# A gated-DeltaNet layer on one core: one dense v tile, 64-row state products in shared PSUM banks, plain matrices for the triangular solve

## Chip, cores and metric

The kernel runs on one core of a Trainium2 chip. The metric is the device time of one execution in microseconds; 3 runs of the kernel before have a median of 1622.08 us (1618.85 to 1623.61). A core has five engines with a queue each: TensorE (PE, its weight loads are listed as PEld), VectorE (DVE), ScalarE (ACT), GpSimd (POOL) and SyncE (SP, which issues the DMAs). They run side by side and meet at semaphores.

## The reference, cut to what matters

Two layers over 256 latent and 256 context tokens of 1024 channels: a state-space layer, then a gated DeltaNet layer, each followed by an MLP. The change lies in the DeltaNet layer, which runs in two directions over 16 value heads in chunks of 64 tokens:

```python
lower = jnp.where(strict, jnp.einsum('nbhcd,nbhsd->nbhcs', k_beta, k_b) * decay, 0.0)
t_mat = lax.linalg.triangular_solve(lower + eye, eye, left_side=True, lower=True, unit_diagonal=True)
u = jnp.einsum('nbhcs,nbhse->nbhce', t_mat, v_b * beta_b[..., None])
w = jnp.einsum('nbhcs,nbhsd->nbhcd', t_mat, k_beta * jnp.exp(g_b)[..., None])
...
def advance(state, w_i, u_i, kend_i, glast_i):
    v_new = u_i - jnp.einsum('bhcd,bhde->bhce', w_i, state)
    new_state = state * jnp.exp(glast_i)[..., None, None] + jnp.einsum('bhcd,bhce->bhde', kend_i, v_new)
    return v_new, new_state
```

For each head and direction there are 8 chunks in a row (4 of context, 4 of latents), so 8 steps that depend on each other.

## The kernel before

Two 64-token chunks, one of each direction, share the 128 partitions: a step n of a head works on chunk n of the forward direction and on its mirror chunk of the backward one, and a chunk sits in rows 0 to 63 or 64 to 127 by its parity. The layer is made of tasks, Python generators that issue instructions piece by piece:

- `gdn_proj` (line 1610): projections from the hidden stream, three fp32r products each (high and low halves of the weights), with `w_load` and `w_split` that load the weights and split them into `whi` (ScalarE) and `wlo` (GpSimd).
- `post_qk`, `post_v`, `post_z` and `prep_kk`: convolution, normalisation and transposes behind the projections.
- `gdn_t` (line 1752): the inverse of the triangular matrix for a pair of heads and one direction, by five doubling steps and two corrections. X is the decay exponent, N the matrix, `nb` its fp16 copy and `lo` the rest. In each doubling step `T` is a transpose of `U` (DVE), `ap` a product with `nb` (TensorE), `A` the masked result (DVE), `up` a product with `A`, and `U` its copy (ACT). `bd` multiplies with a block-diagonal 128 by 128 `nb` in 8 products of 64 columns; `quad` in 16 products of 64 by 64, a row half and a column half each. There are 16 `gdn_t`: 8 pairs, 2 directions.
- `gdn_chain` (line 1837): the recurrence of one head. In a step, `ks` is the product of the key with the state S (`c<-S,kt` in the trace), `r0` the remainder (DVE), `vp` the product of the inverse with r0 (`c<-r,ub`, or `c<-vs,ub` in a head's first step), `v2` its scaled copy (ACT), `kv` the product of the key with v2 (`c<-v,kn`), and the new S two DVE operations on kv. Latent steps add `qs`, `op` and `vn` for the output. Every row of v belongs to one direction; v2 is a 128 by 2 by 128 tile with a column block for each direction, in which the other direction's rows stay zero (`gdn_zero`, line 2041, zeroes these tiles and those of nb and lo once).
- `gdn_out`: the output projection (`wo`), the last work of the layer.

Three chains run at a time (`NCH` is 3), each in a PSUM bank of its own: `self.cp` (line 1491) gives chain x the column blocks ks, kv0 and kv1 of bank `c{x}`. The third bank also serves early projections.

Which task issues next is decided by `drive` (line 323): a model of engine times (`Clock`) finds for each task when its next piece could start, and the earliest one goes, ties by priority (chains 0, solves 1, projections 4, output projection 5). So a change of instructions changes the order of the whole layer on every engine. Each engine then runs its queue in that order. Line 273 is the helper that records every operation, so the trace's rows all carry it and are told apart by tile names.

Of the kernel before, what the change touches and what calls it, by code (L numbers as in the profile page):

```python
# [8 lines left out]
F32 = mybir.dt.float32  # L9
F32R = mybir.dt.float32r  # L10
F16 = mybir.dt.float16
BF16 = mybir.dt.bfloat16
AF = mybir.ActivationFunctionType
OP = mybir.AluOpType
# [1404 lines left out]
M_INC, M_U, M_A, M_ID, M_OFF, M_G, NCONST2 = 0, 128, 256, 896, 960, 1024, 1026  # L1419

NPR, NT, NQK, NCH, NHI, NRB, LZ = 1, 2, 4, 3, 2, 3, 2
# [36 lines left out]
class K3(K2):  # L1458
# [3 lines left out]
    def gdn_init(self, pool):  # L1462

        nc, V, G = self.nc, self.nc.vector, self.nc.gpsimd
        P = self.g = pool
# [7 lines left out]
        for n in range(2):  # L1473
            t = P.tile([128, 524], F32, name=f"pp{n}")
# [11 lines left out]
        for n in range(2):  # L1486
            for L, name in ((self.nb, "nb"), (self.lo, "lo")):
                L.append(P.tile([128, 8, 128], F16, name=f"{name}{n}"))
        self.cb = [self.bank(f"c{n}", f"c{n}", bufs=1) for n in range(3)]

        self.cp = [(b[:, 0:128], b[:, 128:256], b[:, 256:384]) for b in self.cb] + [tuple(b[:, 384:512] for b in self.cb)]
# [6 lines left out]
        for x in range(NCH):  # L1498
            self.v2.append([P.tile([128, 2, 128], F32, name=f"v2{x}{n}") for n in range(2)])
# [252 lines left out]
    def gdn_t(self, p, d, st):  # L1752

        nc, V, G = self.nc, self.nc.vector, self.nc.gpsimd
        W, B, c2 = self.gw, self.gb, self.c2
        tb = lambda name: self.bank(name, f"t{d}", bufs=1)
        B8 = lambda x: x.rearrange("p (c i) -> p c i", i=64)
        B42 = lambda x: x.rearrange("p (m h i) -> p m h i", m=4, h=2)
        mask = lambda n: c2[:, n:n + 64].unsqueeze(1).to_broadcast([128, 8, 64])
        halves = [slice(0, 64), slice(64, 128)]  # L1760

        X = B.tile([128, 512], F32, name="X")
# [5 lines left out]
        G.tensor_tensor(B8(X), B8(X), mask(M_INC + 64 * d), op=OP.add)  # L1768
# [5 lines left out]
        G.tensor_tensor(B8(N), B8(N), mask(M_ID), op=OP.add)  # L1774
# [5 lines left out]
        for h in halves:  # L1780
            nc.scalar.copy(nb[h, :, h], B8(N)[h])
        yield
        for h in halves:
            G.tensor_tensor(lo[h, :, h], B8(N)[h], nb[h, :, h], op=OP.subtract)
        G.tensor_tensor(ibd, B42(X)[:, 2:4], st["kqs"].unsqueeze(2).to_broadcast([128, 2, 2, 64]), op=OP.mult)

        def bd(out, l, r, first, last):
            for b in range(8):
                cs = slice(64 * b, 64 * b + 64)
                nc.tensor.matmul(out[:, cs], l[:, b], r[:, cs], start=first and b == 0, stop=last and b == 7, skip_group_check=True)  # L1790

        def quad(out, l, r):
            for b in range(8):
                cs = slice(64 * b, 64 * b + 64)
                for h in halves:
                    nc.tensor.matmul(out[h, cs], l[h, cs], r[h, cs] if r is not self.id16 else r[h], start=b == 0, stop=b == 7, skip_group_check=True)

        for n in range(5):
            T = B.tile([128, 512], F16, name="T", tag=f"T{d}", bufs=1)
            V.transpose(T, U)  # L1800
            yield
            ap = tb("ap")
            bd(ap, nb, T, True, True)
            A = B.tile([128, 512], F16, name="A", tag=f"A{d}", bufs=1)
            V.tensor_tensor(B8(A), B8(ap), mask(M_A + 64 * (5 * d + n)), op=OP.mult)
            yield
            up = tb("up")
            quad(up, A, U)
            U = B.tile([128, 512], F16, name="U", tag=f"U{d}")
            nc.scalar.copy(U, up)  # L1810
            yield
# [7 lines left out]
        bd(ep, nb, T0, True, False)  # L1819
        bd(ep, lo, T0, False, False)  # L1820
# [16 lines left out]
    def gdn_chain(self, p, h2, st):  # L1837
# [5 lines left out]
        ks, *kv = self.cp[x]  # L1843
# [6 lines left out]
        for n in range(8):  # L1850
# [17 lines left out]
            if n < 7:  # L1868
                v2 = self.v2[x][n % 2]
                for d in range(2):  # L1870
                    nc.scalar.activation(v2[rows[d], d], vp[rows[d]], AF.Identity, scale=self.vsc[rows[d], n, hd:hd + 1])
# [12 lines left out]
            if n < 7:  # L1884
                if x < 3:
                    kvw = self.cb[x][:, 128:384]
                    mm(kvw, kn[:, ms], v2.rearrange("p d e -> p (d e)"))
                else:
                    for d in range(2):
                        mm(kv[d], kn[:, ms], v2[:, d])  # L1890
                Sn = new("S", [128, 2, 128], 2)
                if S is None:
                    if x < 3:
                        nc.scalar.copy(Sn.rearrange("p d e -> p (d e)"), kvw)
                    else:
                        for d in range(2):
                            nc.scalar.copy(Sn[:, d], kv[d])
                else:
                    for d in range(2):
                        V.scalar_tensor_tensor(Sn[:, d], S[:, d], self.egl[:, n, d, hd:hd + 1], kv[d],  # L1900
                                               op0=OP.mult, op1=OP.add)
                S = Sn
                yield
# [137 lines left out]
    def gdn_zero(self):  # L2041

        for t in self.nb + self.lo + [t for v in self.v2 for t in v]:
            self.pin(self.nc.gpsimd.memset(t, 0.0))
            yield

    def gdn_phase(self, tmp, gb, hp, new):
# [56 lines left out]
        zero = T(self.gdn_zero(), 3, [j], "gpsimd")  # L2104
        tasks += [g, zero]
        gates(0)
        for p in range(8):
# [11 lines left out]
            tt.append([T(self.gdn_t(p, d, st[p]), 1, [g, zero, kk] + ago(tt, 1)[d:d + 1] + ago(ch, NRB), "gpsimd") for d in range(2)])  # L2119
# [142 lines left out]
```

## Time and profile before

| | |
|---|---|
| median of 3 runs | 1622.08 us |
| the profiled execution, its own time | 1624.46 us |
| its span, first to last instruction | 1622.7 us |
| granted TensorE clock over the span | 0.947 |
| TensorE busy | 1469.8 us (91%) |
| DVE, ACT, POOL busy | 1096.8, 776.3, 650.6 us |
| recurrence layer | from about 760 to 1421 us |

Times in rows are microseconds from the span's start, unless marked ns. Busy time is the union of an engine's instructions; matmuls are pipelined, so a row's duration is longer than the time until the next one begins, and the difference of two starts tells how long a group holds the engine. An fp32 product is two instructions (two passes) on the chip.

### The profile page before, as it was taken

To read this page: it belongs to the slowest core of one execution; us is meant where nothing else is said; L and a number is where in the kernel's file an instruction comes from. 1 tells how busy PE (TensorE), PEld (TensorE's weight loads), DVE (VectorE), ACT (ScalarE), POOL (GpSimd) and SP (SyncE) were. 2 spreads that over 40 slices of the span, in tenths; PEclk is the share of its full clock that TensorE was granted. 3 is DMA by queue.
4 is the path that set the end of the run, shared out by engine and by line. 5 is a ranking of instruction groups with operands and counts; after the bars stand their busy time and mean duration, and the time that the engine had idled before them with its cause. 6 is when DMAs were issued, how large, how long until landed. Compare 5 with 4: busy or idle time off the path is not lost. (4 is left out here: it accounts for less than half of the span.)

```text
span 1622.7 us, 31318 instructions
## 1 busy us (share of the span) xinstructions
PE 1469.8 (91%) x12370; PEld 1115.6 (69%) x12370; DVE 1096.8 (68%) x2036; ACT 776.3 (48%) x1635; POOL 650.6 (40%) x590
## 2 busy tenths in 40 slices
PE   6898558999999999997978898989998999989998
PEld 2355436777777788886767676767776665689997
DVE  6978858774334344447999967686978875667766
ACT  3243456553223232325556655656675755554543
POOL 3962003642333233334776734353544400024432
PEclk7999779998999999998979999989998999999999
DMA  9887743554455533322222211111111102536552
GB/s 274 290 270 250 110 91 132 173 192 146 139 173 178 177 118 104 104 78 81 93 66 66 66 53 60 40 60 44 56 63 57 41 25 96 196 121 198 181 193 91
DMA packets 76771, 200.77 MB, mean 124 GB/s; under 512 B 8784, under 2 KB 29008, under 8 KB 76368
## 3 DMA queue, kind: packets, MB, share of 16 engines
q1 hardware_dynamic: 76112, 197.78, 38.5%
q8 instruction: 97, 1.59, 0.4%
q10 hardware_dynamic: 512, 0.98, 0.3%
q14 instruction: 50, 0.41, 0.1%
HBM read 192.71 MB, written 6.03 MB: 122 GB/s over the span
## 5 line engine op out<-in xcount | busy, mean ns | idle before, releaser
L273 ACT CAST whi<-wraw 128x1024 fp32r<-128x1024 f32 x221 | 225.3, 1045 | 239.5 <-PE w L273 149.2
L273 POOL TENSOR_TENSOR wlo<-wraw,whi 128x256 fp32r<-128x256 f32 (+1 forms) x221 | 208.3, 970 | 289.5 <-ACT whi L273 271.9
L273 DVE TENSOR_TENSOR wlo<-wraw,whi 128x1024 fp32r<-128x1024 f32 (+1 forms) x189 | 225.1, 1220 | 61.7 <-ACT whi L273 60.3
L273 PE MATMUL w<-hh,whi 128*128 128x256 f32 (+1 forms) x512 | 169.9, 335 | 0.0
L273 PE MATMUL w<-hl,whi 128*128 128x256 f32 (+1 forms) x512 | 168.9, 331 | 0.0
L273 PE MATMUL w<-hh,wlo 128*128 128x256 f32 (+1 forms) x512 | 168.4, 331 | 0.4 <-DVE wlo L273 0.4
L273 PE MATMUL w<-whi,h1l 128*128 128x512 f32 x384 | 148.4, 390 | 0.0
L273 PE MATMUL w<-wlo,h1h 128*128 128x512 f32 x384 | 148.4, 389 | 0.0
L273 POOL TENSOR_TENSOR sq<-rl 128x512 f32<-128x512 f32 (+1 forms) x64 | 62.4, 975 | 213.7 <-ACT rl L273 213.7
L273 PE MATMUL w<-whi,h1h 128*128 128x512 f32 x384 | 147.7, 393 | 0.0
L273 PE MATMUL proj<-hh,whi 128*128 128x256 f32 (+1 forms) x360 | 132.4, 368 | 7.4 <-ACT pp L273 6.7
L273 DVE TENSOR_TENSOR ma<-w,g 128x512 f32<-128x512 f32 x96 | 65.3, 687 | 105.3 <-PE w L273 105.2
L273 PE MATMUL proj<-hh,wlo 128*128 128x256 f32 (+1 forms) x360 | 127.5, 354 | 1.3 <-POOL wlo L273 1.3
L273 PE MATMUL proj<-hl,whi 128*128 128x256 f32 (+1 forms) x360 | 127.5, 354 | 0.0
L273 DVE SCALAR_TENSOR_TENSOR cacc<-pp,cw,cacc 128x520 f32<-128x520 f32 (+1 forms) x128 | 112.4, 879 | 9.6 <-ACT cacc L273 8.1
L273 POOL TENSOR_TENSOR xr<-xr,ma 128x512 f32<-128x512 f32 x56 | 79.5, 1421 | 89.2 <-DVE ma L273 89.2
L273 DVE TENSOR_TENSOR h1l<-sq,h1h 128x512 fp32r<-128x512 f32 (+1 forms) x64 | 35.5, 555 | 114.4 <-POOL sq L273 111.9
L273 ACT ACTIVATE v<-c,vsc 64x128 f32<-64x128 f32 x224 | 80.7, 362 | 62.4 <-PE c L273 57.6
L273 PEld LDWEIGHTS w<-hh,whi 128*128 128x128 f32 x512 | 98.0, 192 | 14.9 <-DVE wlo L273 2.5
L273 PEld LDWEIGHTS w<-hl,whi 128*128 128x128 f32 x512 | 98.2, 192 | 10.7 <-issue 1.9
L273 PEld LDWEIGHTS w<-hh,wlo 128*128 128x128 f32 x512 | 97.9, 192 | 10.2 <-issue 0.8
L273 ACT ACTIVATE rl<-w 128x512 f32<-128x512 f32 (+1 forms) x64 | 31.3, 489 | 130.1 <-PE w L273 120.8
(316 smaller groups left out, 3480.2 us busy)
## 6 DMA issues: line engine op xcount, KB each, us to landing
wraw<-in_w_dram SPq DMA_DIRECT2D x128, 512.0 KB, 4.3
adaw<-in_ada_w_dram SPq DMA_DIRECT2D x92, 512.0 KB, 4.8
wraw<-in_w_in_dram SPq DMA_DIRECT2D x48, 512.0 KB, 3.2
wraw<-in_w_glu_dram SPq DMA_DIRECT2D x32, 512.0 KB, 3.3
wraw<-in_w_out_dram SPq DMA_DIRECT2D x16, 512.0 KB, 3.5
Kt<-kd SPq DMA_DIRECT2D x32, 128.0 KB, 6.2
X<-grd SPq DMA_DIRECT2D x32, 128.0 KB, 3.2
V<-in_ada_w_dram SPq DMA_DIRECT2D x4, 512.0 KB, 6.1
```

Of the source, the lines that this page charges most:

```text
L273: r = f(*args, **kw)
```

## The change

1. `v2` becomes a dense 128 by 128 tile, filled by one activation. The state product is made for each direction apart, from the 64 rows of its chunk, into 128 columns.
2. The banks are dealt out anew: `c2` holds ks and vp of all three chains (128 columns each), `c0` the states of chunks of even parity and `c1` those of odd parity, again for all three chains.
3. `nb` and `lo` become plain 128 by 512 tiles, and `bd` is gone: `quad` does all products of the solve. One ScalarE copy makes nb.
4. GpSimd's additions on X and N and its `lo` are done in pieces of 256 columns.
5. `gdn_zero` and its task are gone.

```diff
-                L.append(P.tile([128, 8, 128], F16, name=f"{name}{n}"))
+                L.append(P.tile([128, 512], F16, name=f"{name}{n}"))
...
-        self.cp = [(b[:, 0:128], b[:, 128:256], b[:, 256:384]) for b in self.cb] + [tuple(b[:, 384:512] for b in self.cb)]
+        self.cp = [tuple(self.cb[n][:, 128 * x:128 * x + 128] for n in (2, 0, 1)) for x in range(NCH)]
...
-            self.v2.append([P.tile([128, 2, 128], F32, name=f"v2{x}{n}") for n in range(2)])
+            self.v2.append([P.tile([128, 128], F32, name=f"v2{x}{n}") for n in range(2)])
...
+        quarters, two = [slice(0, 256), slice(256, 512)], [slice(0, 4), slice(4, 8)]
...
-        G.tensor_tensor(B8(X), B8(X), mask(M_INC + 64 * d), op=OP.add)
+        for b in two:
+            G.tensor_tensor(B8(X)[:, b], B8(X)[:, b], mask(M_INC + 64 * d)[:, b], op=OP.add)
...
-        G.tensor_tensor(B8(N), B8(N), mask(M_ID), op=OP.add)
+        for b in two:
+            G.tensor_tensor(B8(N)[:, b], B8(N)[:, b], mask(M_ID)[:, b], op=OP.add)
...
-        for h in halves:
-            nc.scalar.copy(nb[h, :, h], B8(N)[h])
+        nc.scalar.copy(nb, N)
         yield
-        for h in halves:
-            G.tensor_tensor(lo[h, :, h], B8(N)[h], nb[h, :, h], op=OP.subtract)
+        for c in quarters:
+            G.tensor_tensor(lo[:, c], N[:, c], nb[:, c], op=OP.subtract)
...
-        def bd(out, l, r, first, last):
-            for b in range(8):
-                cs = slice(64 * b, 64 * b + 64)
-                nc.tensor.matmul(out[:, cs], l[:, b], r[:, cs], start=first and b == 0, stop=last and b == 7, skip_group_check=True)
...
-            bd(ap, nb, T, True, True)
+            quad(ap, nb, T)
...
-        bd(ep, nb, T0, True, False)
-        bd(ep, lo, T0, False, False)
+        quad(ep, nb, T0, True, False)
+        quad(ep, lo, T0, False, False)
...
-                for d in range(2):
-                    nc.scalar.activation(v2[rows[d], d], vp[rows[d]], AF.Identity, scale=self.vsc[rows[d], n, hd:hd + 1])
+                nc.scalar.activation(v2, vp, AF.Identity, scale=col(self.vsc, n))
...
-                if x < 3:
-                    kvw = self.cb[x][:, 128:384]
-                    mm(kvw, kn[:, ms], v2.rearrange("p d e -> p (d e)"))
...
+                kv = [kvs[c % 2] for c in cs]
+                for d in range(2):
+                    mm(kv[d], kn[rows[d], ms], v2[rows[d]])
...
-        for t in self.nb + self.lo + [t for v in self.v2 for t in v]:
-            self.pin(self.nc.gpsimd.memset(t, 0.0))
-            yield
```

The order on TensorE, late in the layer, where chains stand close together. The names are those of the trace with the tile's number: c0 to c2 are the banks, S, r0, vs and v2 carry the chain's number (S2 is a state of chain 2, v201 a v2 of chain 0), and an fp32 product is one row here. Before, with three chains:

```order
L273 MATMUL c0_6466<-S0_15218,kt_12408 64x128 [waits DVE_49]
L273 MATMUL c0_6466<-S0_15218,kt_12408 64x128
L273 MATMUL c2_6468<-S2_15456,kt_13768 64x128 [waits Activation_49]
L273 MATMUL c2_6468<-S2_15456,kt_13768 64x128
L273 MATMUL c1_6467<-S1_15127,kt_12408 64x128 [waits DVE_49]
L273 MATMUL c1_6467<-S1_15127,kt_12408 64x128
L273 MATMUL qs_15181<-S1_15127,qt_12456 64x128 [waits DVE_49]
L273 MATMUL qs_15181<-S1_15127,qt_12456 64x128
L273 MATMUL op_15227<-vn0_15189,ibd0_13117 64x128 [waits DVE_49]
L273 MATMUL op_15227<-vn0_15189,ibd1_13798 64x128
L273 MATMUL c0_6466<-r00_15248,ub0_13893 64x128 [waits DVE_49]
L273 MATMUL c0_6466<-r00_15248,ub1_14627 64x128
```

In this stretch every chain writes its own bank and waits for one engine, the one that made its state or remainder.

The change, at the corresponding place, with the last two heads' chains:

```order
L273 MATMUL c2_6468<-S2_16357,kt_15009 64x128 [waits DVE_49,Activation_49]
L273 MATMUL c2_6468<-S2_16357,kt_15009 64x128 [waits DVE_49]
L273 MATMUL c1_6467<-v201_6470,kn_14878 128x128
L273 MATMUL c0_6466<-v201_6470,kn_14878 128x128
L273 MATMUL c2_6468<-r02_16380,ub0_16126 64x128 [waits DVE_49]
L273 MATMUL c2_6468<-r02_16380,ub1_16257 64x128
L273 MATMUL c2_6468<-S0_16384,kt_15009 64x128 [waits DVE_49,Activation_49]
L273 MATMUL c2_6468<-S0_16384,kt_15009 64x128 [waits DVE_49]
L273 MATMUL c0_6466<-v220_6473,kn_14878 128x128
L273 MATMUL c1_6467<-v220_6473,kn_14878 128x128
```

Both chains write ks and vp into c2. The first product with S of one chain now waits for DVE (its state) and for ACT (the other chain's v2, which ACT reads from c2). The state product is two rows into two banks.

The order on GpSimd, in the first solves. Before:

```order
L273 TENSOR_TENSOR N_7259<-N_7259,c2_6444 128x512 [waits DVE_49]
L273 TENSOR_TENSOR ibd0_7296<-X_7168,kqs_7132 128x256 [waits Activation_49]
L273 TENSOR_TENSOR ibd1_7301<-X_7171,kqs_7132 128x256
L273 TENSOR_TENSOR N_7268<-N_7268,c2_6444 128x512 [waits DVE_49]
L273 TENSOR_TENSOR lo0_6463<-N_7259,nb0_6462 64x8x64 [waits Activation_49]
L273 TENSOR_TENSOR lo0_6463<-N_7259,nb0_6462 64x8x64 [waits Activation_49,Pool_49]
L273 TENSOR_TENSOR X_8109<-X_8109,c2_6444 128x512 [waits DMAHW7_49,DMAHW6_49,Pool_49]
L273 TENSOR_TENSOR lo1_6465<-N_7268,nb1_6464 64x8x64 [waits Activation_49]
L273 TENSOR_TENSOR lo1_6465<-N_7268,nb1_6464 64x8x64 [waits Activation_49,Pool_49]
```

Here an addition on X or N is one row, and `lo` one row for each half of the partitions (in this listing c2_6444 is the table of masks, not a bank).

The change:

```order
L273 TENSOR_TENSOR N_7161<-N_7161,c2_6444 128x256 [waits DVE_49]
L273 TENSOR_TENSOR N_7161<-N_7161,c2_6444 128x256
L273 TENSOR_TENSOR N_7219<-N_7219,c2_6444 128x256 [waits DVE_49]
L273 TENSOR_TENSOR N_7219<-N_7219,c2_6444 128x256
L273 TENSOR_TENSOR X_8061<-X_8061,c2_6444 128x256 [waits DMAHW6_49,DMAHW5_49,Pool_49]
L273 TENSOR_TENSOR X_8061<-X_8061,c2_6444 128x256
L273 TENSOR_TENSOR lo0_6463<-N_7161,nb0_6462 128x256 [waits Activation_49]
L273 TENSOR_TENSOR lo0_6463<-N_7161,nb0_6462 128x256 [waits Pool_49]
```

All three are two rows of 256 columns over all partitions.

## Rows read from the trace of the kernel before

**Rows 1.** The page, busy time of TensorE (us, share of the span, instructions).

```profile
PE 1469.8 (91%) x12370; PEld 1115.6 (69%) x12370; DVE 1096.8 (68%) x2036; ACT 776.3 (48%) x1635; POOL 650.6 (40%) x590
```

**Rows 2.** Stretches: length; PE, PEld, DVE, ACT, POOL busy; clock; DMA share; GB/s.

```profile
760.00:840.00 80.00, 68.99 (x378) 58.06 (x377) 74.52 (x106) 41.17 (x91) 59.99 (x69) 0.91 0.27 87
840.00:1337.00 497.00, 455.88 (x5576) 338.21 (x5575) 390.82 (x827) 307.53 (x800) 230.29 (x242) 0.95 0.16 52
...
1350.00:1397.00 47.00, 44.87 (x273) 27.60 (x273) 26.99 (x74) 24.58 (x63) 1.71 (x2) 1.00 0.33 111
```

**Rows 3.** TensorE in order of time from 1254 us: start, duration, group.

```profile
1254.52 0.70 PE L273 MATMUL c<-v,kn 128*128 128x256 f32 x2
1255.15 0.43 PE L273 MATMUL op<-vn,ibd 64*64 64x128 f32 x4
1255.42 0.39 PE L273 MATMUL c<-r,ub 64*64 64x128 f32 x4
1255.74 0.44 PE L273 MATMUL c<-S,kt 128*64 128x128 f32 x4
1256.11 0.44 PE L273 MATMUL up<-U,A 64*64 64x64 f16 x16
1256.47 0.32 PE L273 MATMUL qs<-S,qt 128*64 128x128 f32 x1
...
1257.07 0.41 PE L273 MATMUL ap<-T,nb 128*128 128x64 f16 x8
1257.31 0.68 PE L273 MATMUL c<-v,kn 128*128 128x256 f32 x2
...
1262.31 0.41 PE L273 MATMUL ap<-T,nb 128*128 128x64 f16 x8
1262.64 0.43 PE L273 MATMUL c<-r,ub 64*64 64x128 f32 x4
```

**Rows 4.** The same view near 1094 us.

```profile
1094.22 0.59 PE L273 MATMUL c<-v,kn 128*128 128x256 f32 x2
1094.75 0.44 PE L273 MATMUL op<-vn,ibd 64*64 64x128 f32 x4
```

**Rows 5.** What TensorE waited for, 840 to 1397: us, times, longest us.

```profile
PE ap L273 <- DVE T L273: 12.8, 7, 4.5
PE c L273 <- DVE S L273: 9.5, 8, 4.8
...
PE c L273 <- DVE r L273: 3.8, 4, 2.6
PE c L273 <- ACT vn L273: 3.3, 6, 1.1
...
PE c L273 <- ACT v L273: 3.1, 7, 0.7
```

**Rows 6.** ScalarE's groups, 760 to 1400: busy us, mean ns, idle before.

```profile
L273 ACT ACTIVATE v<-c,vsc 64x128 f32<-64x128 f32 x224 | 80.7, 362 | 62.4 <-PE c L273 57.6 <-DVE cacc L273 2.0 <-DVE qss L273 0.2
...
L273 ACT CAST nb<-N 64x512 f16<-64x512 f32 x32 | 19.7, 617 | 6.5 <-POOL N L273 3.1 <-PE ep L273 2.9
```

**Rows 7.** GpSimd's groups, 760 to 1345, the same columns.

```profile
L273 POOL TENSOR_TENSOR wlo<-wraw,whi 128x256 fp32r<-128x256 f32 x184 | 152.2, 858 | 153.4 <-ACT whi L273 136.0 <-PE ap L273 9.8 <-PE kTp L273 7.2
...
L273 POOL TENSOR_TENSOR N<-N,c 128x512 f32<-128x512 f32 x16 | 23.7, 1499 | 4.0 <-DVE N L273 4.0
L273 POOL TENSOR_TENSOR X<-X,c 128x512 f32<-128x512 f32 x16 | 22.7, 1426 | 6.7 <-DMA X<-grd 5.1 <-PE kp L273 1.2
...
L273 POOL MEMSET nb<- 128x1024 f16 x2 | 1.9, 1002 | 0.0
L273 POOL MEMSET lo<- 128x1024 f16 x2 | 1.9, 950 | 0.0
L273 POOL MEMSET v<- 128x256 f32 x6 | 1.6, 308 | 0.0
```

**Rows 8.** State products from 1337 to 1421, the groups of TensorE.

```profile
L273 PE MATMUL c<-v,kn 128*128 128x256 f32 x34 | 10.9, 403 | 1.7 <-ACT vn L273 0.9 <-ACT v L273 0.6
```

More of the change, by code (lines that the diff above doesn't have):

```diff
@@ L1779, in gdn_t, with quad @@
         nb, lo = self.nb[d], self.lo[d]
-        for h in halves:
-            nc.scalar.copy(nb[h, :, h], B8(N)[h])
+        nc.scalar.copy(nb, N)
         yield
-        for h in halves:
-            G.tensor_tensor(lo[h, :, h], B8(N)[h], nb[h, :, h], op=OP.subtract)
+        for c in quarters:
+            G.tensor_tensor(lo[:, c], N[:, c], nb[:, c], op=OP.subtract)
         G.tensor_tensor(ibd, B42(X)[:, 2:4], st["kqs"].unsqueeze(2).to_broadcast([128, 2, 2, 64]), op=OP.mult)
-        def bd(out, l, r, first, last):
-            for b in range(8):
-                cs = slice(64 * b, 64 * b + 64)
-                nc.tensor.matmul(out[:, cs], l[:, b], r[:, cs], start=first and b == 0, stop=last and b == 7, skip_group_check=True)
-        def quad(out, l, r):
+        def quad(out, l, r, first=True, last=True):
             for b in range(8):
@@ L1795, in quad @@
                 for h in halves:
-                    nc.tensor.matmul(out[h, cs], l[h, cs], r[h, cs] if r is not self.id16 else r[h], start=b == 0, stop=b == 7, skip_group_check=True)
+                    nc.tensor.matmul(out[h, cs], l[h, cs], r[h, cs] if r is not self.id16 else r[h],
+                                     start=first and b == 0, stop=last and b == 7, skip_group_check=True)
         for n in range(5):
@@ L1842, in gdn_chain @@
         x = (2 * p + h2) % NCH
-        ks, *kv = self.cp[x]
+        ks, *kvs = self.cp[x]
         vp = ks
@@ L1884, in gdn_chain @@
             if n < 7:
-                if x < 3:
-                    kvw = self.cb[x][:, 128:384]
-                    mm(kvw, kn[:, ms], v2.rearrange("p d e -> p (d e)"))
-                else:
-                    for d in range(2):
-                        mm(kv[d], kn[:, ms], v2[:, d])
+                kv = [kvs[c % 2] for c in cs]
+                for d in range(2):
+                    mm(kv[d], kn[rows[d], ms], v2[rows[d]])
                 Sn = new("S", [128, 2, 128], 2)
                 if S is None:
[L1893 to L1897, printed above, removed]
+                    for d in range(2):
+                        nc.scalar.copy(Sn[:, d], kv[d])
                 else:
@@ L2039, in tail_init @@
         self.end = end
-    def gdn_zero(self):
-        for t in self.nb + self.lo + [t for v in self.v2 for t in v]:
-            self.pin(self.nc.gpsimd.memset(t, 0.0))
-            yield
     def gdn_phase(self, tmp, gb, hp, new):
@@ L2103, in gdn_phase @@
         tasks.append(T(alone(), 0, [j], "gpsimd"))
-        zero = T(self.gdn_zero(), 3, [j], "gpsimd")
-        tasks += [g, zero]
+        tasks.append(g)
         gates(0)
@@ L2118, in gdn_phase @@
                 v.append(T(self.post_v(p, h2, st[p], x), 3, [j] + ago(ch, NRB), "scalar"))
-            tt.append([T(self.gdn_t(p, d, st[p]), 1, [g, zero, kk] + ago(tt, 1)[d:d + 1] + ago(ch, NRB), "gpsimd") for d in range(2)])
+            tt.append([T(self.gdn_t(p, d, st[p]), 1, [g, kk] + ago(tt, 1)[d:d + 1] + ago(ch, NRB), "gpsimd") for d in range(2)])
             for h2 in range(2):
```

## Prediction

> **What bounds the kernel now.** I began with the page. TensorE is busy for 91% of the span [rows 1], an average over stages that says nothing of the stage that is changed. So I cut the second half into stretches by what is recorded there [rows 2]: 760 to 840 us (first projections and gates), 840 to 1337 (recurrence layer with all its helpers), and 1350 to 1397 (last chains beside output projection). In the first DVE is the full one, 74.5 of 80 us. From 840 to 1397 TensorE is: 455.9 of 497 and 44.9 of 47 us, with DVE at 79% and ACT at 62% in the former. The granted clock there is 0.95, so a tenth of the time ran at 1.2 GHz and the rest at 2.4.
>
> What does TensorE's busy time consist of? Starts of successive groups in the order of time show it [rows 3]. A group of four `c<-S` (two directions, two passes each, on two column halves of the array) holds the engine for 0.37 us until the next group begins; sixteen `up` (64 by 64, fp16) 0.36; eight `ap` (full array, fp16) 0.24 when a full-array product comes next and 0.33 when a 64 by 64 one does. The state product `c<-v,kn`, one of 112, holds it for 0.63 us, the dearest step of a chain. A quieter place has 0.53 [rows 4]. Half of that product's columns meet zeros: each v row is filled for one direction, so the full 128 by 256 product does twice the needed work.
>
> When TensorE idles, it is mostly for DVE [rows 5]: 12.8 us before `ap` for the transpose, 9.5 for S. The waits of the chains (S, r, vn, v) are 19.7 us together, at 25 places.
>
> **The change part by part.** All is against the profiled execution, 1624.46 us (span 1622.7); the median of the runs, 1622.08, lies 2.4 lower.
>
> State product: 112 products of 128 rows by 256 columns become 224 of 64 rows by 128 columns, one per direction, in two banks. No row of this trace has two products on the two row halves. The nearest are `c<-S` (two column halves, 0.37 for both directions) and `op` (64 by 64 on the diagonal, 0.27 until the next group in the same mode) [rows 3]; in both the two directions run beside each other. If row halves do the same, a group goes from between 0.53 and 0.63 down to 0.37: 112 x 0.16 = 18 us to 112 x 0.26 = 29 us less. If the second has to follow the first, it takes 0.37 + 0.27 = 0.64, which is 1 us (against 0.63) to 12 us (against 0.53) more. I take **-23 us**, the middle of the first pair, since every pair of half-size products in the rows overlaps.
>
> Solve products on plain matrices: `ap` goes from 8 full products to 16 quarter ones, 80 times. Like `up` it will hold 0.36 us, today 0.24 to 0.33: +0.03 x 80 = +2 to +0.12 x 80 = +10. `ep` has two such sets 16 times: 2 x (0.36 - 0.24) x 16 = +4 at most, and less since the second set follows in the same mode. I take **+6** for both, since most `ap` stand beside 64-row groups as in the rows, with 14 as the upper end. The Trainium skill (TensorEngine Tiling (Array Packing), section Key Properties) says that a change of tiling mode drains TensorE. The 0.24 and 0.33 of `ap` agree. By that rule alone every `ap` beside a projection pays a switch it does not pay now, which is the +14 end, and the sum below would be 8 us poorer.
>
> ScalarE: 224 activations of v on 64 rows, 362 ns each, become 112 on 128 rows; the 32 copies of N into nb (617 ns each) become 16 [rows 6]. That is 40.5 and some 10 us of ACT time, nearly all beside TensorE's work: TensorE idled 3.1 us for v and 3.3 for vn, queued behind v [rows 5]. I take **-2**, between 0 and -6.4. The first state copy of a head is split in two, 16 times, a few hundred ns, under the same cover. If ACT were late, kn's product would be the next one to wait.
>
> GpSimd: N and X are added in two pieces of 256 columns. A piece of 256 has 858 ns (`wlo`), a whole one 1499 and 1426 [rows 7]: +0.22 and +0.29 us on each solve's path, which the copy into nb gives back (-0.62, one activation in place of two). `lo`, now two pieces over 128 rows in place of two over 64, is read only by `ep`, a dozen steps later. Sum on the path -0.1 us for each of 16 solves in two lanes: **0**, with 16 x 0.5 / 2 = 4 us either way. Shorter pieces might also hold up DVE less; the rows price only whole instructions.
>
> Zeroing: ten memsets, 1.9 + 1.9 + 1.6 = 5.4 us [rows 7], vanish from GpSimd's queue while DVE sets the pace [rows 2]: **-1**, between 0 and -5.4. No DMA is added or taken away.
>
> Banks: until now every chain had a bank of its own. Now c2 holds ks and vp of all three chains, and c0 and c1 their states. A TensorE write into a bank waits for reads of it that stand earlier, whichever columns they take. In the instruction order 62 in place of 16 `c<-S` wait for ACT, 29 in place of 0 `c<-r`, 7 in place of 4 `c<-vs`, and 34 in place of 0 state products wait for DVE: 46 + 29 + 3 + 34 = 112 waits more. What is queued behind them on TensorE is everything. Price: the order of before has 112 waiting `c<-S`, 112 `c<-r` and 112 state products, and these 336 cost 19.7 us of idling [rows 5], 0.06 each; so 112 x 0.06 = **+7**. From below it is 0 (each already over), from above 112 x 0.36 (a whole read of v) = +41.
>
> Sum: -23 + 6 - 2 + 0 - 1 + 7 = -13, 1611 us for the profiled execution, **1609** against the median.
>
> **The rivals.**
> *Chain latency counts as well.* One step loses a v activation (0.36) and the longer end of the state product (0.26): 0.62 us x 7 steps x 16 heads / 3 lanes = 23 us on top, 1586. For it: TensorE's idling before state products is all for v and vn [rows 5]. Against it: from 840 on TensorE is over 90% busy, so a chain that is ready sooner finds the engine taken.
> *The freed time isn't collected.* DVE, on which TensorE waits most, gets no less work. Then only the stretch from 1337, where no projection of the layer is left and output projection soon fills the gaps, gives its part: 17 state products (34 instructions [rows 8]) x 0.26 = 4 us, 1618. Within 0.3% (about what a measurement of this kernel can tell from no change, 4.9 us).
> *Shared banks stall the engine (slower).* Place: ks of one chain behind the v read of another, as in the order shown above, where two heads strictly alternate on c2. If each new wait costs the whole 0.36 us read, 41 in place of 7: 1643. It decides from (13 + 7) / 112 = 0.18 us a wait, three times what a chain's wait costs now. Against it: a read is over in 0.36 us and other work stands between most pairs. For it: ACT has `whi` casts of a microsecond in its queue ahead of v. The Trainium skill (PSUM — Partial Sum Buffer, section on bank collisions) asks to guard PSUM by bank and quadrant and not by address; that is why disjoint columns don't help, and the order's waits agree.
> *Row halves run one after the other (slower).* The state product then gains nothing (+1 in place of -23) and `ap` stays dearer: 1633. Against it stands every overlapping pair in the rows; none is of this kind, though.
>
> **How the numbers follow.** Forecast (1609) 0.45; latency as well (1586) 0.12; not collected (1618) 0.17; stalls from banks (1643) 0.16; row halves in turn (1633) 0.10. Faster: 0.45 + 0.12 = 0.57; same 0.17; slower 0.16 + 0.10 = 0.26. The range leaves out the 0.16 of full stalls and reaches from just under the latency case to the case of row halves in turn: 1585 to 1634, which also takes in the bounds of `ap` and `ep` (+8 more), of the zeroing and of GpSimd. The faster cases by themselves span 1585 to 1617.
>
> **What would show it.** Right: a state-product group of four instructions that holds TensorE for about 0.37 us; `ap` with 16 at 0.36; v with 112 activations of some 0.36 us; TensorE's idling for chains (S, r, v, vn) within some 7 us of today's 19.7. Wrong: if the pairs of state products start 0.27 us apart, row halves don't overlap; if idling before `c<-S` and `c<-r` for ACT reaches 20 us, banks have eaten the gain; if TensorE's busy time from 840 falls by 15 us or more and the time doesn't, DVE holds the pace.

## The result, and the profile after

The changed kernel takes **1733.87 us** (median of 4 runs, 1728.69 to 1736.18) against 1622.84 for the kernel before on the same chip: a ratio of 1.0682, 95% interval 1.0649 to 1.0715, 111 us slower. The prediction, 1609 us and most likely faster, was wrong in sign, and the time lies outside its range. The profiled execution took 1733.88 us, with a span of 1732.1.

First the stretches of the changed kernel (length; PE, PEld, DVE, ACT and POOL busy; granted clock; DMA share; GB/s). The second stretch runs from 840 us to the last state of the last chain, the third from there into the layer that follows:

```profile
760.00:840.00 80.00, 65.69 (x384) 55.71 (x384) 72.78 (x110) 41.28 (x96) 54.78 (x64) 0.88 0.24 80
840.00:1487.00 647.00, 573.42 (x7012) 413.32 (x7010) 407.84 (x901) 282.33 (x759) 217.31 (x270) 0.87 0.14 46
1487.00:1630.00 143.00, 134.38 (x792) 116.91 (x792) 94.84 (x138) 72.43 (x121) 35.72 (x35) 0.96 0.53 177
```

The kernel before, from 840 us to its own last state:

```profile
840.00:1389.00 549.00, 504.95 (x5911) 368.48 (x5912) 419.49 (x911) 335.32 (x878) 231.30 (x243) 0.96 0.18 58
```

The recurrence layer is where the time went: 549 us have become 647, 98 of the 111. Nothing got busier but TensorE; DVE, ACT and POOL are busy for less. TensorE's idle time grows from 549 - 505 = 44 us to 647 - 573 = 74, which is 30 us. Its busy time grows by 68. The granted clock says why: it is the mean of full and half speed (2.4 and 1.2 GHz), so twice what is missing to 1 is the share of time at 1.2 GHz. Before that was 2 x 0.04 x 549 = 44 us, after it is 2 x 0.13 x 647 = 168 (the clock has two digits, so each is good to some 6 us). At 1.2 GHz a group of four `c<-S` holds TensorE for 0.63 us against 0.37 (medians of 16 and 55 groups of this trace with no idling behind them, start to start), and a 512-column projection product for 0.43 against 0.23: 1.7 to 1.85 times as long. So 124 us more at 1.2 GHz is worth an estimated 51 to 57 us, most of the 68.

What TensorE waited for from 840 to 1487 us (us, times, longest), to be held against [rows 5]:

```profile
PE c L273 <- ACT v L273: 16.8, 31, 1.4
PE up L273 <- DVE A L273: 12.2, 13, 2.8
PE c L273 <- DVE r L273: 12.1, 23, 1.1
PE ap L273 <- DVE T L273: 10.9, 17, 1.4
...
PE c L273 <- DVE S L273: 0.8, 2, 0.5
...
PE c L273 <- ACT vn L273: 0.4, 1, 0.4
```

The waits of the chains (S, r, vn, v) rose from 19.7 to 30.1 us and changed their names: fewer for S, many more for v and r. How that comes about is seen at the end of the layer, where two chains are left. All engines of the changed kernel in order of time:

```profile
1440.84 0.35 DVE L273 SCALAR_TENSOR_TENSOR r<-c,neg,vs 128x128 f32<-128x128 f32 x1 [1.29 <-PE c L273]
...
1441.36 0.69 PE L273 MATMUL c<-r,ub 64*64 64x128 f32 x4
1441.46 0.61 DVE L273 SCALAR_TENSOR_TENSOR S<-S,egl,c 128x128 f32<-128x128 f32 x2 [0.27 <-PE c L273]
1442.10 0.37 ACT L273 ACTIVATE v<-c,vsc 128x128 f32<-128x128 f32 x1 [2.15 <-DVE S L273]
...
1442.52 0.70 PE L273 MATMUL c<-S,kt 128*64 128x128 f32 x4 [0.47 <-ACT v L273]
...
1443.14 0.80 PE L273 MATMUL c<-v,kn 64*128 64x128 f32 x4
1443.36 0.35 DVE L273 SCALAR_TENSOR_TENSOR r<-c,neg,vs 128x128 f32<-128x128 f32 x1 [1.29 <-PE c L273]
...
1443.87 0.69 PE L273 MATMUL c<-r,ub 64*64 64x128 f32 x4
1443.97 0.61 DVE L273 SCALAR_TENSOR_TENSOR S<-S,egl,c 128x128 f32<-128x128 f32 x2 [0.27 <-PE c L273]
1444.61 0.37 ACT L273 ACTIVATE v<-c,vsc 128x128 f32<-128x128 f32 x1 [2.15 <-DVE S L273]
```

One chain has its new S at 1442.07 (1441.46 + 0.61). Its `c<-S` starts at 1442.52, when the *other* chain's v has been read out of the shared bank (1442.10 + 0.37). So the two chains strictly alternate, one step every 2.51 us, now of one and now of the other, and neither works in the other's pauses. In the kernel before two chains with banks of their own go side by side: eight instructions in one group (two chains, two directions, two passes), and no wait for the other chain's read. That stretch runs at 2.4 GHz and has output projection (`wo`) between the steps, so it is not the lengths that can be compared but who waits for whom:

```profile
1353.95 0.66 PE L273 MATMUL c<-S,kt 128*64 128x128 f32 x8
...
1354.44 0.61 DVE L273 SCALAR_TENSOR_TENSOR r<-c,neg,vs 128x128 f32<-128x128 f32 x2 [0.39 <-PE c L273]
...
1354.84 0.69 PE L273 MATMUL c<-r,ub 64*64 64x128 f32 x8 [0.24 <-DVE r L273]
```

What the clock does there, and somewhat earlier (stretches of the changed kernel, columns as above):

```profile
1355.00:1358.40 3.40, 3.40 (x48) 3.10 (x47) 2.46 (x9) 2.77 (x10) 0.34 (x1) 1.00 0.00 1
1358.40:1361.80 3.40, 2.43 (x38) 1.53 (x33) 1.70 (x5) 1.65 (x9) 3.40 (x5) 1.00 0.04 10
1361.80:1365.20 3.40, 2.99 (x14) 1.91 (x12) 0.17 (x1) 3.25 (x14) 0.02 (x1) 0.75 0.46 154
1365.20:1395.00 29.80, 26.29 (x270) 17.36 (x271) 17.66 (x37) 10.69 (x27) 10.35 (x12) 0.51 0.05 15
1395.00:1400.00 5.00, 4.68 (x88) 3.40 (x81) 3.83 (x9) 1.93 (x6) 0.00 (x0) 1.00 0.09 26
...
1420.00:1425.00 5.00, 5.00 (x101) 4.08 (x95) 3.69 (x11) 0.74 (x3) 0.00 (x0) 1.00 0.18 56
1425.00:1428.00 3.00, 2.42 (x52) 1.74 (x44) 2.51 (x6) 1.67 (x5) 2.09 (x4) 1.00 0.00 0
1428.00:1432.00 4.00, 2.86 (x18) 1.75 (x19) 0.52 (x2) 3.04 (x12) 1.71 (x3) 0.97 0.37 131
1432.00:1470.00 38.00, 34.41 (x145) 16.86 (x145) 11.26 (x32) 5.71 (x17) 0.00 (x0) 0.50 0.02 8
```

TensorE runs full and at 2.4 GHz until 1425, is busy for 2.42 of 3 and 2.86 of 4 us while the last chains begin to wait, and from 1432 runs at 1.2 GHz for 38 us. It is then "busy" for 91% of the time: at half speed the products themselves fill the pauses. The same goes on some 70 us before: full until 1358, busy for 2.43 of 3.4 us, then nearly 30 us at 1.2 GHz, and 2.4 again from 1395.

What the change set out to do did happen. The state product in the changed kernel, TensorE in order of time:

```profile
1269.97 0.49 PE L273 MATMUL c<-v,kn 64*128 64x128 f32 x4
1270.39 0.44 PE L273 MATMUL op<-vn,ibd 64*64 64x128 f32 x4
```

A group of four (two directions, two passes) holds the engine for 0.42 us, where one product held it for 0.53 to 0.63 [rows 3, 4]; the median of 89 such groups is the same 0.42. ScalarE and GpSimd, from 760 us on (busy us, mean ns, idle before):

```profile
L273 ACT ACTIVATE v<-c,vsc 128x128 f32<-128x128 f32 x100 | 36.7, 367 | 73.6 <-PE c L273 57.2 <-PE ap L273 4.9 <-PE tp L273 4.7
...
L273 ACT CAST nb<-N 128x512 f16<-128x512 f32 x16 | 10.0, 624 | 10.0 <-POOL N L273 9.7 <-PE ep L273 0.2
```
```profile
L273 POOL TENSOR_TENSOR N<-N,c 128x256 f32<-128x256 f32 x32 | 28.3, 913 | 14.5 <-DVE N L273 14.5
L273 POOL TENSOR_TENSOR X<-X,c 128x256 f32<-128x256 f32 x32 | 26.6, 856 | 5.8 <-DMA X<-grd 5.4 <-POOL N L273 0.2
```

These are the sizes that the prediction took [rows 6, 7], and the memsets of nb, lo and v are gone.

### The profile page after: what moved, and what is told of

Read it like the earlier page. It is cut to its first block, busy times and chain, and to the rows that moved or that the text cites. A ratio compares the mean times of both kernels' runs of the same rounds, so it can differ in the third digit from the quotient of the medians.

```text
span 1732.1 us, 33546 instructions
## 1 busy us (share of the span) xinstructions
PE 1547.8 (89%) x13490; PEld 1166.2 (67%) x13490; DVE 1087.2 (63%) x2036; ACT 725.8 (42%) x1523; POOL 631.4 (36%) x612
## 4 chain that ended last, share of the span: by engine, by line
PE 66%; DVE 15%; DMA 6%; ACT 5%; issue 4%; POOL 3%; SPq 1%; ACTq 0%; POOLq 0%; DVEq 0%
PE w L273 30%; PE proj L273 8%; PE c L273 7%; PE ada L273 4%; DVE cacc L273 3%; PE wo L273 2%; PE glu L273 2%; DMA wraw<-in_w_dram 1%; POOL wlo L273 1%; PE qs L273 1%; PE op L273 1%; PE xin L273 1%; PE up L273 1%; PE ap L273 1%; ACT whi L273 1%
## 5 line engine op out<-in xcount | busy, mean ns | idle before, releaser
L273 POOL TENSOR_TENSOR wlo<-wraw,whi 128x256 fp32r<-128x256 f32 (+1 forms) x221 | 203.2, 946 | 396.5 <-ACT whi L273 380.8
L273 PE MATMUL proj<-hh,whi 128*128 128x256 f32 (+1 forms) x360 | 136.6, 379 | 5.3 <-DVE zs L273 3.6
L273 PE MATMUL proj<-hh,wlo 128*128 128x256 f32 (+1 forms) x360 | 131.2, 364 | 1.3 <-POOL wlo L273 1.3
L273 DVE SCALAR_TENSOR_TENSOR cacc<-pp,cw,cacc 128x520 f32<-128x520 f32 (+1 forms) x128 | 104.1, 814 | 8.5 <-ACT cacc L273 6.9
L273 DVE SCALAR_TENSOR_TENSOR S<-S,egl,c 128x128 f32<-128x128 f32 x192 | 59.1, 340 | 67.5 <-PE c L273 66.7
L273 PEld LDWEIGHTS proj<-hh,whi 128*128 128x128 f32 x360 | 76.2, 212 | 17.6 <-DVE zs L273 4.2
```

The lines of the kernel that those rows point to most:

```text
L273: r = f(*args, **kw)
```

## The experiments

Five theories. **Banks**: chains that share PSUM banks hold each other up. **Half rows**: products on half of the array's rows bring the clock down by themselves. **Solve**: the quads and GpSimd's pieces cost the time. **Planner**: its prices for the new shapes, or its whole-bank rule, order the layer badly. **New order**: any edit reorders the whole layer, and the order of before is hard to match. Three chains run at a time (NCH = 3); where an expectation speaks of four lanes, of a chain 3 or of "three chains of four", it miscounts: that chain doesn't exist, and the price of 28 steps is that of 37.

### One part at a time

*The solve alone* (of the change, only what stands in the solve):

```
-                L.append(P.tile([128, 8, 128], F16, name=f"{name}{n}"))
+                L.append(P.tile([128, 512], F16, name=f"{name}{n}"))
...
-            bd(ap, nb, T, True, True)
+            quad(ap, nb, T)
...
```

> The kernel before with the solve of the change alone: plain nb and lo, 64x64 quads in ap and ep, one copy of nb, GpSimd in 256 columns, nb and lo not zeroed; chains, zero-padded v and banks as before. Banks theory (chains that share banks hold each other up, 0.1 us and more per step): nothing of the loss is here, 1615 to 1630 us. Half-row theory (a product that fills half of the array's rows lets the granted clock fall, and time with it): part of the loss, since 1,280 products go from full rows to a quarter of the array; 1640 to 1680 us, with more time at 1.2 GHz between 840 and 1400 us. Planner theory (the planner prices a quad at twice its real time and orders the layer badly): 1640 us or more too, but with the clock unchanged in stretches that are equally busy.

1658.54 us, ratio 1.0212 (1.0197 to 1.0227): +34. The banks theory had left nothing for the solve (1615 to 1630), so it misses here; the half-row and the planner theories don't.

*The chain alone* (dense v, 64-row products, banks by parity; bd and zeroed nb and lo stay):

```
...
-  mm(kvw, kn[:, ms], v2.rearrange("p d e -> p (d e)"))
+  mm(kv[d], kn[rows[d], ms], v2[rows[d]])
...
```

> The kernel before with the chain of the change alone: dense v, 64-row state products, banks by chunk parity; the solve as before, with zeroed nb and lo. Banks theory: all of the loss is here, 1710 to 1740 us. Half-row theory: part of the loss, 1640 to 1690 us, with a lower granted clock. Planner theory: near the time before, 1610 to 1640 us, since the modelled time of a state product is the same.

1732.39 us, ratio 1.0661 (1.0642 to 1.068): all of the loss. The solve's edits, which cost 34 us alone, add 1.5 on top of it, which can't be told from nothing. Its layer:

```profile
840.00:1497.00 657.00, 572.25 (x6136) 406.27 (x6134) 426.21 (x908) 292.93 (x773) 234.79 (x245) 0.86 0.15 48
```

*The banks alone* (v stays padded, products keep 128 rows):

```
-  self.cp = [(b[:, 0:128], b[:, 128:256], b[:, 256:384]) for b in self.cb] + [tuple(b[:, 384:512] for b in self.cb)]
+  self.cp = [tuple(self.cb[n][:, 128 * x:128 * x + 128] for n in (2, 0, 1)) for x in range(NCH)]
...
-  mm(kvw, kn[:, ms], v2.rearrange("p d e -> p (d e)"))
...
+  kv = [kvs[c % 2] for c in cs]
+  for d in range(2):
+      mm(kv[d], kn[:, ms], v2[:, d])
...
```

> The kernel before with the banks of the change alone: all chains' reads and v in the third bank, states by chunk parity in the other two; v stays padded with zeros and the state products keep their 128 rows (two of 128 columns instead of one of 256 in three chains of four). Banks theory: as slow as the chain alone, 1700 us or more. Half-row theory: close to the time before, 1615 to 1640 us, with the clock as before, since the rows are full. The difference between this and the chain alone is then what half rows cost.

1741.1 us, ratio 1.072 (1.0698 to 1.0742). Full rows, no quads, no dense v, and it is the slowest of the three:

```profile
840.00:1501.00 661.00, 577.59 (x6119) 425.95 (x6119) 434.00 (x909) 341.21 (x893) 225.93 (x242) 0.89 0.15 47
```

Idle 83 us and 145 us at 1.2 GHz. Half rows are not needed for either. With them (the chain alone) idling is as long, 85 us, there are 2 x 0.14 x 657 = 184 us at 1.2 GHz, and the time is 9 us less, which is as little as a new order moves (below).

*The changed kernel, planned as before*: the planner takes a quad pair of `ap` and `ep` at the full product's time, and counts the state product as full rows.

```
+  if self.as_bd:
+      stream /= 2
-  self.count(start, end, n * passes * ins[0].ap[0][1] / 128)
+  self.count(start, end, n * passes * (1 if self.full else ins[0].ap[0][1] / 128))
```

> The changed kernel with one thing else: the planner prices each ap and ep quad as the full-row product it replaced, and counts the state products' activity as full rows, so that it orders the layer by the costs of the kernel before; the instructions on the chip are those of the change. Planner theory: most of the loss goes, 1620 to 1660 us. Banks and half-row theories: within 15 us of the changed kernel, 1715 to 1750 us.

1731.96 us, ratio 1.0672 (1.0641 to 1.0703): nothing changed. The planner's prices for the new shapes are not the cause.

### Waits on the chip, or the order made for them

*Split products*: the kernel before with two products of 128 columns per state, in the banks of before, so that it differs from the banks alone in the place of the columns, and in the order that the planner makes of it.

```
-  mm(kvw, kn[:, ms], v2.rearrange("p d e -> p (d e)"))
...
+  for d in range(2):
+      mm(kv[d], kn[:, ms], v2[:, d])
...
```

> The kernel before with the state products of three chains split in two of 128 columns (and the first states' copies in two), in the banks of before: it differs from the banks-alone kernel in where the chains' columns lie and in nothing else. Banks theory: the time before, 1618 to 1640 us. If the split itself (twice as many products and issues) carries the loss: 1700 us or more.

1646.47 us, ratio 1.0143 (1.0101 to 1.0184). The split itself is 23 us, which leaves the time 6 us over what the banks theory had allowed. The rest of the banks-alone kernel's loss, 1741.1 - 1646.5 = **95 us, is sharing**, good to what a new order does (below). Its layer:

```profile
840.00:1399.00 559.00, 507.82 (x6102) 388.95 (x6100) 409.43 (x900) 336.13 (x888) 233.17 (x244) 0.96 0.16 52
```

Idle 51 us, at 1.2 GHz for 45. Sharing added 32 us of idling and 100 us at half speed, the same two entries as in the change itself.

*The two crossed*: the planner reckons with one set of banks, the chip has the other.

```
+    def seen(self, ap):
...
+        k, s = self.other(self.virt[n], a // 128)
+        return "c%d" % k, (128 * s + a % 128, 128 * s + a % 128 + b - a)
```

> The split products in the banks of before, but the planner reckons as if the chains lay in the banks of the change, so that the priorities are those of the banks-alone kernel while the waits on the chip are those of before. If the loss comes from waits for shared banks on the chip: at most 1650 us. If it comes from the order that the planner makes under its whole-bank rule: 1700 us or more.

> The banks-alone kernel (shared banks on the chip), but the planner reckons as if the chains lay in the banks of before. Waits on the chip: within 20 us of the banks-alone kernel, 1720 to 1760 us, or more. Planner's order: 1620 to 1660 us.

1647.32 us (ratio 1.0132, 1.0102 to 1.0163) and 1743.82 us (1.073, 1.0687 to 1.0773). The banks that the planner believes in make no difference; those on the chip make all of it, 96.5 us between the two. One reserve: neither kernel got the other's order. In the traces VectorE's order in a crossed kernel agrees with the one that it was to copy in about two thirds of its groups, no better than a null variant's (below) does with that of before. What is shown is that two different orders with banks apart, and two with shared banks, take the same time each.

### Other banks for the changed kernel

*Ring*: a bank is shared by two chains.

```
-  self.cp = [tuple(self.cb[n][:, 128 * x:128 * x + 128] for n in (2, 0, 1)) for x in range(NCH)]
+  B = [[b[:, 128 * n:128 * n + 128] for n in range(4)] for b in self.cb]
+  self.cp = [(B[x][0], B[x][1], B[(x + 1) % 3][2]) for x in range(3)] + [tuple(b[3] for b in B)]
```

> The changed kernel with other banks: chains 0 to 2 keep their reads, v and one state half in a bank of their own, the other state half lies in the next chain's bank, and chain 3 has one slot in each, so that a bank is shared by three chains and no bank takes the reads and v of all four. Banks theory: part of the loss goes, 1650 to 1710 us. Half-row theory: as the changed kernel, 1720 to 1745 us.

1701.18 us, ratio 1.0471 (1.0442 to 1.05): 33 us of the loss are gone. Its layer idles for 44 us and has 2 x 0.12 x 615 = 148 us at 1.2 GHz:

```profile
840.00:1455.00 615.00, 571.41 (x6949) 419.13 (x6949) 407.72 (x892) 277.76 (x752) 216.72 (x265) 0.88 0.15 47
```

*Turned*: each bank has one chain's reads and v, and a state half of each of the two others.

```
+  self.cp = [(B[x][0], B[(x + 1) % 3][1], B[(x + 2) % 3][2]) for x in range(3)] + [tuple(b[3] for b in B)]
```

> The changed kernel with its banks turned: chains 0 to 2 have reads and v in banks 0 to 2 and their two state halves in the two others, chain 3 a slot in each. Every bank is shared by all four chains as in the change, but no bank takes the reads and v of all. If the one bank of reads and v is what holds the chains up: 1650 to 1700 us. If it is sharing as such: 1715 to 1745 us. Half-row theory: 1720 to 1745 us.

1705.24 us, ratio 1.0521 (1.0489 to 1.0553), between the two expectations: the bank that takes every read and v is some 30 us of the loss (new orders differ among each other by up to 14, below), the rest stays with both other ways of sharing. Its layer and its waits for v and S:

```profile
840.00:1459.00 619.00, 572.66 (x6945) 418.37 (x6937) 403.90 (x889) 275.93 (x751) 214.01 (x265) 0.87 0.15 47
```
```profile
PE c L273 <- DVE S L273: 8.1, 16, 1.5
PE c L273 <- ACT v L273: 8.0, 14, 1.5
```

Here something stays open, for the ring as well. Idling, 46 us, is that of before, and the chains' waits are too (19.6 us); yet 2 x 0.13 x 619 = 161 us run at 1.2 GHz. Half speed hides pauses in busy time, as at the end of the layer above, so this may be the banks still. Or half rows, which are in both kernels, do lower the clock where banks are shared: the chain alone has 184 us at 1.2 GHz, the banks alone 145 with the same idling. A kernel with turned banks and full rows would tell, and wasn't tried.

### The solve's pieces

*Quads without GpSimd's pieces*, *the pieces alone*, and *the solve alone with the full product's price in the planner*:

```
...
-  for b in two:
-      G.tensor_tensor(B8(X)[:, b], B8(X)[:, b], mask(M_INC + 64 * d)[:, b], op=OP.add)
+  G.tensor_tensor(B8(X), B8(X), mask(M_INC + 64 * d), op=OP.add)
...
```

(N and lo likewise; the second kernel has the same lines in the other direction on the kernel before, for X and N; the third has the `as_bd` lines above.)

> The kernel before with plain nb and lo and 64x64 quads in ap and ep, but GpSimd's X and N additions whole and lo in two pieces of 64 rows as before: the solve-alone kernel less its GpSimd pieces. If the quads carry the solve's loss (34 us alone): 1650 to 1665 us. If the GpSimd pieces do: 1620 to 1632 us.

> The kernel before with one thing changed: GpSimd's additions on X and N in two pieces of 256 columns. If the quads carry the solve's loss: 1618 to 1632 us. If the GpSimd pieces do (each of 16 solves one step later): 1645 us or more.

> The solve-alone kernel, but the planner prices each ap and ep quad as the full-row product it replaced. If the solve's loss is the planner's (it holds 640 pairs to be twice as long as they are): 1620 to 1640 us. If it is the chip's (pairs of quads that really take longer, or idle more of the array): 1650 to 1665 us.

1685.05 us (1.0385, 1.0365 to 1.0405), 1642.81 (1.0136, 1.0106 to 1.0166) and 1670.82 (1.0301, 1.0276 to 1.0326). None of the three lies in a range that was expected, and they don't add up: quads 62, pieces 20, both together 34; and the planner's price, once "mended", makes it worse. That was the hint to the fifth theory. The clock of the layer is 0.94 in these three and in the solve alone, 68 to 72 us at 1.2 GHz. The pieces, with the products of before, have as much of it as the quads (before: 44), so it isn't the quads' shape that brings it.

### Nothing but a new order

Three kernels with the instructions of before, in each of which the planner's fixed price of one engine's instruction is up by 1 ns:

```
-  cost = (66 - 4 * psum + n * (...)) / 960
+  cost = (67 - 4 * psum + n * (...)) / 960
...
-  cost = 0.15 + 2.1 * n / 1000
+  cost = 0.151 + 2.1 * n / 1000
...
-  cost = (0.051 if psum else 0.093) + 0.093 * extra + n / 1200
+  cost = (0.052 if psum else 0.094) + 0.093 * extra + n / 1200
```

> The kernel before with the planner's fixed price of a VectorE instruction raised by 1 ns, and nothing else: the same instructions in another order. If an order made anew costs what the small edits cost: 1640 to 1660 us. If the edits themselves cost it: 1618 to 1630 us.

> The kernel before with the planner's fixed price of a GpSimd instruction raised by 1 ns, and nothing else. If an order made anew costs what the small edits cost: 1640 to 1660 us. If the edits themselves cost it: 1618 to 1630 us.

> The kernel before with the planner's fixed price of a ScalarE instruction raised by 1 ns, and nothing else. If an order made anew costs what the small edits cost: 1640 to 1660 us. If the edits themselves cost it: 1618 to 1630 us.

1644.62 us (1.0148, 1.0123 to 1.0174), 1631.04 (1.0048, 1.0033 to 1.0063) and 1642.04 (1.0118, 1.0098 to 1.0137): **9 to 23 us slower for no edit at all**. So the 20 us of the pieces, the 23 of the split and the 9 between half and full rows can't be told from a new order; of the quads' 62 some 40 can, as far as three orders tell.

### Longer steps, with waits and with work

*v read twice*, in the banks of before:

```
-  for d in range(2):
+  for d in (0, 1, 0, 1):
       nc.scalar.activation(v2[rows[d], d], vp[rows[d]], AF.Identity, scale=self.vsc[rows[d], n, hd:hd + 1])
```

> The kernel before with each v read from PSUM twice, so that every chain's step is 0.73 us longer, with its own banks as before: no chain waits for another. If a chain's own latency is what the layer pays for (28 steps in a row on each of four lanes, 20 us): 1635 to 1655 us. If the shared banks cost by holding up TensorE's queue and the other chains, and latency alone is mostly hidden: 1622 to 1635 us.

1692.43 us, ratio 1.0423 (1.0394 to 1.0452), more than either expectation. With three lanes 112 x 0.73 / 3 = 27 us of steps in a row cost 69, or 46 to 60 without the new order. Its layer:

```profile
840.00:1459.00 619.00, 542.95 (x5909) 385.44 (x5908) 430.07 (x909) 413.99 (x1102) 228.81 (x242) 0.91 0.16 51
```

Idle 76 us, 2 x 0.09 x 619 = 111 us at 1.2 GHz: the signature of the change, with its shapes and its banks left out. ACT's queue is longer too (414 us busy against 335), so this doesn't price a chain's latency by itself.

*State products issued twice*, the second over the first, in the kernel before and in the changed one:

```
+  mm(kvw, kn[:, ms], v2.rearrange("p d e -> p (d e)"))
...
-  for d in range(2):
+  for d in (0, 1, 0, 1):
       mm(kv[d], kn[rows[d], ms], v2[rows[d]])
```

> The kernel before with each state product issued twice, the second over the first: some 0.43 us more TensorE work per step, 48 us in all, in the banks of before. If the clock falls when TensorE waits: the granted clock stays at 0.945 or above, and the time is the work and a new order, 1665 to 1690 us. If longer steps as such bring the clock down (as in the kernel whose v is read twice, 0.931): a clock of 0.935 or less and 1690 us or more.

> The changed kernel with each 64-row state product issued twice, the second over the first: 0.42 us more TensorE work per step, 47 us in all, in the shared banks. If the clock falls when TensorE waits, and added work keeps it up: a granted clock above the changed kernel's 0.909 and less than 30 us over its time, 1735 to 1763 us. If not: the clock as there, and 1770 to 1800 us.

The first takes 1696.34 us (1.0464, 1.0443 to 1.0486), 73 more, of which 48 are the work and 9 to 23 a new order; it is 6 us over the range that was expected with a clock that stays up, and the clock of the execution, 0.952, did stay up. Its layer:

```profile
840.00:1453.00 613.00, 555.18 (x6111) 408.23 (x6111) 419.95 (x904) 336.40 (x876) 230.37 (x244) 0.96 0.15 48
```

Steps longer by TensorE's own work leave the clock where it was, 0.96, with 49 us at 1.2 GHz. The second takes 1745.93 us (1.0754, 1.0722 to 1.0785), only 12 more than the changed kernel for 47 us of added products:

```profile
840.00:1496.00 656.00, 583.94 (x7443) 434.87 (x7443) 411.76 (x897) 281.85 (x756) 218.47 (x270) 0.91 0.15 46
```

Time at 1.2 GHz falls from 168 to 118 us, and the clock of the execution rises from 0.909 to 0.927. By the lengths above, 50 us less at 1.2 GHz gives back an estimated 21 to 23 of the 35 us that the added work doesn't cost; the rest is within what a new order does.

## Why the prediction was wrong

**The step that failed is the price of the banks**, "112 x 0.06 = +7", with "112 x 0.36 (a whole read of v) = +41" as its upper end. The mechanism and the place were right: `c<-S` of one chain does wait for v of another. Measured, sharing costs 95 us, 0.85 for each of the 112 waits counted in the instruction order, over twice the bound. The banks-alone kernel, on which the 95 rest, still reads v twice a step, 0.73 us; even that bound would be 112 x 0.73 = 82. The chain alone, with the one read that I counted, is 108 us slower than the kernel before, its cheaper state products included. The mean idling of a waiting chain product, [rows 5] over 336, was the wrong row to take the price from. As I read it, a chain that waits in the kernel before leaves TensorE to two others that don't depend on it, while shared banks tie the three together, so that all wait at once; the end of the layer shows this for two chains, for three it is argued. And the bound counted one read, not what follows when TensorE stops.

The Trainium skill (Perfetto Trace Analysis, section Matmuls) asks that independent groups rotate through different banks, so that the read of one lies beside the products of the next. The split products against the banks alone agree with it, and put 95 us on it.

**What follows is the clock, and no term of the sum and no rival held it.** I read 0.95 from [rows 2] and carried it over. Two thirds of the layer's growth (68 of 98 us) is busy time of TensorE, and half speed accounts for an estimated 51 to 57 of it. Steps made longer by reads brought the clock down (twice-read v, 111 us at 1.2 GHz, with more work for ACT besides), steps made longer by products did not (twice issued, 49), and in the changed kernel 47 us of products cost 12. That pauses are the reason is borne out by this, and by the two falls of the clock shown above, but it isn't the whole of it: the ring and the turned banks idle no longer than the kernel before and still have 148 and 161 us at 1.2 GHz. What brings the clock down there stays open, and half rows haven't been ruled out as a part of it.

The Trainium skill (TensorE: Matmul & The Clock Gate, section on psum-queue depth-cycling) tells of a kernel whose short pauses between groups, while it cycles through PSUM banks, let the clock alternate between its two levels. The stretches from 1355 to 1470 us agree: 1.00, 0.51, 1.00, 0.50. By that rule the change had a rival that I didn't weigh.

**A new order was no part of the sum either.** 9 to 23 us for a price off by 1 ns say that a sum of -13 had no ground here: the gain that I forecast is smaller than what two of the three null orders cost.

The other terms, in the order of the prediction:
- *State product, -23*: the row halves do overlap. A group takes 0.42, not 0.37, so the engine's own saving is 112 x 0.11 = 12 to 112 x 0.21 = 24 us. With shared banks the half-row kernel is 9 us faster than the full-row one, within what a new order does, so none of it is seen for sure in the time. Row halves in turn (1633) falls.
- *`ap` and `ep`, +6*: sixteen `ap` hold TensorE for 0.37 us, start to start, in the median of 40 groups (said: 0.36). In the changed kernel all of the solve's edits together are 1.5 us; alone they cost 34, of which a new order may be 9 to 23. Where the remainder arises isn't settled.
- *ScalarE, -2; GpSimd, 0; zeroing, -1*: the durations hold (367, 624, 913 and 856 ns), and the freed 53 us of ACT in the layer (335 to 282) bought nothing that shows.
- *Latency counts as well (1586)*: steps made longer cost more than the 23 us by which I priced steps made shorter. That shorter ones gain wasn't shown.
- *Freed time not collected (1618)*: it isn't collected, but DVE is not what paces: it is busy for 63% of the layer after, 76% before.
- *Shared banks stall the engine (1643)*: the right rival, with a price too small by 90 us.

**Two of the signs that I named were blind.** I asked for 20 us of idling before `c<-S` and `c<-r` for ACT as the sign that banks ate the gain. The groups of the changed kernel's layer show 3.3 and 3.8:

```profile
L273 PE MATMUL c<-v,kn 64*128 64x128 f32 x448 | 73.4, 359 | 9.1 <-ACT v L273 7.8 <-DVE S L273 0.8 <-ACT S L273 0.3
...
L273 PE MATMUL c<-S,kt 128*64 128x128 f32 x444 | 66.0, 330 | 7.2 <-DVE r L273 3.6 <-ACT v L273 3.3
...
L273 PE MATMUL c<-r,ub 64*64 64x128 f32 x444 | 54.0, 323 | 12.2 <-DVE r L273 8.3 <-ACT v L273 3.8
```

Those are 7.1 of the 74 us that TensorE idles in the layer, and at half speed pauses turn into busy time: one `c<-S` instruction has a median of 273 ns at 2.4 GHz in both kernels and of 421 at 1.2 GHz in the changed one, where 99 of 444 run at that speed and 16 did before. And TensorE's busy time, which I wanted to see fall, rose. The sign that did speak was the plain one: chain waits "within some 7 us of today's 19.7" are 30.1.

No version came out faster than the kernel before; of those in which chains share banks the ring is the best, 4.7% above it.

## What to carry to other kernels

Where a few independent chains keep an in-order TensorE fed, count the PSUM banks that each has to itself before counting columns saved: a bank shared by two chains makes one wait for the other's reads, and that can cost far more than the read (here 0.85 us a wait, against 0.36 a read and 0.73 for both reads of a step), part of it through the clock. Price any edit that adds pauses to a nearly full TensorE with the time it may spend at 1.2 GHz, and read the granted clock of the stretch beside its busy time, since busy time at half speed looks like work. Where an order is computed from prices, run two or three null variants first; their spread is the least that an edit must gain to be seen.

## What I had not expected of the hardware

- 47 us of useless TensorE work cost 12 us, while the granted clock rose from 0.909 to 0.927 (a new order is in the 12 as well).
- Two 64-row fp32 products on the two row halves, in different banks, take 0.42 us for both directions, against 0.37 for two products on column halves [rows 3].
- Reads from PSUM are no slower in shared banks: v on 64 rows takes 362 ns in the mean in the banks alone and 362 before [rows 6], and v on 128 rows 367 in the changed kernel. The cost is in who waits, not in the access.
